# The gate of the second channel group moved into its state-space loop, two token blocks at a time

## The chip, the cores and the metric

The kernel runs on one core of a Trainium2 chip. It is one program for the core's engines: TensorE (PE, matrix products; PEld is its weight loads), VectorE (DVE), ScalarE (ACT), GpSimd (POOL), and SyncE (SP), which here only issues DMA transfers. The metric is the device time of one execution in microseconds (us); a time given for a kernel is the median of its runs.

## The reference, cut to what matters

The reference is one decoder layer over 1024 tokens of width 1024, in float32: two token mixers side by side, an output projection, a layer norm, a feed-forward part. One input projection feeds both mixers. The change is in the first mixer, a chunked state-space scan with a gate:

```
proj = x @ w_in
z, xbc, dt_raw, q, k, v, qi, ki, wi = jnp.split(proj, offsets, axis=-1)
xbc = jax.nn.silu(_causal_dwconv(xbc, ssd_conv_w, ssd_conv_b))
...
y = _ssd_scan(xs, dt, a, bm, cm)              # 8 chunks of 128 tokens, 2 groups of 8 heads
y = y + d_skip[:, None] * xs
gy = y.reshape(bsz, seqlen, SSD_INNER) * jax.nn.silu(z)
gy = gy.reshape(bsz, seqlen, SSD_GROUPS, SSD_INNER // SSD_GROUPS)
gy = gy * lax.rsqrt(jnp.mean(jnp.square(gy), axis=-1, keepdims=True) + RMS_EPS)
y_ssd = gy.reshape(bsz, seqlen, SSD_INNER) * ssd_norm_g
...
y_att = _dsa_attention(q, k, v, qi, ki, wi)   # each query attends to its 256 best keys
return jnp.concatenate([y_ssd, y_att], axis=-1) @ w_out
```

The gate is the product with silu(z) and the norm behind it. It is taken token by token, so the gate of a token block needs only the scan's result of that block; the norm needs a mean over the 512 channels of one group, for one token.

## The kernel before

A matrix product in float32 is done as three products of rounded halves (`three`, L156 to L159): an operand is split into a high part (`w_hi`) and a low part (`w_lo`). For weights of the input projection a DMA brings `w_raw`, and GpSimd computes `w_hi` (L127) and `w_lo` (L130). Results go through DRAM from stage to stage: `z_dr` holds z, `y_dr` the gated scan, `q_dr`, `k_dr`, `v_dr` the attention's operands.

The stretch that matters is the last stage of the input projection, from about 480 to 640 us. Three streams of work run in it, woven in turn, one step of each per round by `par`. The first is the plan `STAGES[4]`: the last two z tiles, the v tile (per 128-token block a `tps` product, which ScalarE brings out as `tout`), then q tiles 5, 6 and 7 in halves of 512 tokens (`proj`, brought out by ScalarE as `qkout`; tiles 6 and 7 are woven together). The second, `k_load`, starts 11 rounds late and loads the keys (`kraw`), which ScalarE and VectorE split into `kh` and `kl`. The third is the scan of the second channel group, `ssd_gen(1)`, with priority over the rest, and behind it the gate, `gate_gen(1)`.

The scan has 8 chunks of 128 tokens, here called c0 to c7, of two steps each. The first step loads a row of sums (`acsb`, a DMA); ScalarE makes the decay matrix `lmat` of it (8 relu and one exp, L523 and L525), VectorE masks it (L530), and GpSimd makes `xdt`, `xdd` and `skip`. The second does three products on TensorE (`yoff` L542, `stps` L548, `yps` L558), carries the state on (L551, L552), and VectorE writes the chunk's y (L560).

The gate goes over the 8 token blocks, b0 to b7: a DMA loads `zs` (L569), ScalarE takes silu (L570), VectorE multiplies (L572), ScalarE squares and sums (`sq`, L574). It yields after every second block. Then come the square root (L578), the reciprocal, the scaling of all 8 blocks (L582), and four steps that transpose (`yT`, L588) and store y. After the stage, the first part of the output projection starts (`ops`), with weights split by ScalarE (L129).

The order in which TensorE, VectorE, ScalarE and GpSimd take their instructions is set by a scheduler, from dependences and priorities. SP is left in the order of the program: a transfer that waits there holds every transfer behind it. Buffers come from pools with a fixed count: `xdt`, `xdd`, `skip`, `off`, `state`, `zs` and `sq` share five buffers ("s2", by `mid`), `w_raw`, `kraw`, `qraw`, `vraw` and `y_raw` share three ("wr"), and the projection products share two PSUM banks ("ip"). A transfer into a buffer waits until the last user of that buffer is through. ScalarE holds the table of one function set at a time; where exp, silu and square root follow each other, the program has an `ACT_TABLE_LOAD` between them.

Of the kernel before, what the change touches and what calls it, by code (L numbers as in the profile page):

```python
# [32 lines left out]
SSD_PRIO = 100  # L33
KDEL = 11
# [10 lines left out]
WAS = 1  # L45
TPT = ('tp', 'tp', 'ip')
QP = 2
CHAINS = (((7, "act"), (6, "dve")), ((5, "act"), (2, "act"), (4, "dve"), (3, "dve")))


# [7 lines left out]
def hybrid_layer(ctx, tc, x, w_in, ssd_conv_w, ssd_conv_b, dt_bias, a_log, d_skip, ssd_norm_g,  # L58
# [444 lines left out]
    def hv(t):  # L503
        return t.rearrange("p (h n) -> p h n", h=8)

    def ssd_gen(g, tag):
        dt, acs, eacs, cd, dd = decays
        bt, ct = bc[8 + g], bc[10 + g]
        state = None
        for c in range(NB):  # L510
            cs = slice(c * P, (c + 1) * P)
            if c % 4 == 0:
                ps = bank("btp", "tp")
                for j in range(4):
                    nc.tensor.transpose(ps[:, j * P:(j + 1) * P], bt[:, (c + j) * P:(c + j + 1) * P], ident)
                btok = mid("btok", shape=(P, 4, P))
                nc.scalar.activation(btok, ps.rearrange("p (j n) -> p j n", j=4), AF.Copy)
            ab = big("acsb", tag=tag, shape=(P, 8, P))
            nc.sync.dma_start(ab, bass.AP(tensor=a_dr.tensor, offset=a_dr.offset + (c * 16 + g * 8) * P,
                                          ap=[[0, P], [P, 8], [1, P]]))  # L520
            lm = big("lmat", tag=tag, shape=(P, 8, P))
            for h in range(8):
                nc.scalar.activation(lm[:, h, :], ab[:, h, :], AF.Relu, bias=acs[:, c, g * 8 + h:g * 8 + h + 1],  # L523
                                     scale=-1.0)
            nc.scalar.activation(lm, lm, AF.Exp, scale=-1.0)  # L525
            ps = bank("cbps", "tp")
            nc.tensor.matmul(ps[:, :P], bt[:, cs], ct[:, cs], start=True, stop=True)
            cb = small("cbm", (P, P))
            nc.vector.tensor_tensor(cb, ps[:, :P], tri, op=OP.mult)
            nc.vector.tensor_tensor(lm, lm, cb[:, None, :].to_broadcast([P, 8, P]), op=OP.mult)  # L530
            xc = xs[g][c // 2][:, c % 2, :]
            xd = [mid("xdt"), mid("xdd") if c < NB - 1 else None]
            nc.gpsimd.tensor_tensor(hv(xd[0]), hv(xc), heads(dt, g, c), op=OP.mult)
            if c < NB - 1:
                nc.gpsimd.tensor_tensor(hv(xd[1]), hv(xc), heads(dd, g, c), op=OP.mult)
            skip = mid("skip")
            nc.gpsimd.tensor_tensor(hv(skip), hv(xc), dsk[:, g * 8:g * 8 + 8][:, :, None].to_broadcast([P, 8, 64]),
                                    op=OP.mult)
            yield
            if c:  # L540
                po = bank("yoff", "lg")
                nc.tensor.matmul(po, ct[:, cs], state, start=True, stop=True)  # L542
                off = mid("off")
                nc.vector.tensor_tensor(hv(off), hv(po), heads(eacs, g, c), op=OP.mult)
                nc.gpsimd.tensor_tensor(skip, skip, off, op=OP.add)
            if c < NB - 1:
                pst = bank("stps", "lg")
                nc.tensor.matmul(pst, btok[:, c % 4, :], xd[1], start=True, stop=True)  # L548
                new = mid("state")
                if c:  # L550
                    nc.gpsimd.tensor_tensor(hv(new), hv(state), heads(cd, g, c), op=OP.mult)  # L551
                    nc.vector.tensor_tensor(new, new, pst, op=OP.add)  # L552
                else:
                    nc.vector.tensor_copy(new, pst)
                state = new
            py = bank("yps", "lg")
            for h in range(8):
                nc.tensor.matmul(py[:, h * 64:h * 64 + 64], lm[:, h, :], xd[0][:, h * 64:h * 64 + 64],  # L558
                                 start=True, stop=True)
            nc.vector.tensor_tensor(xc, py, skip, op=OP.add)  # L560
            yield


    def gate_gen(g):
        ssq = small("ssq", (P, NB))
        for b in range(NB):
            bs = slice(b * P, (b + 1) * P)
            zs = mid("zs")
            nc.sync.dma_start(zs, z_dr[bs, g * 512:g * 512 + 512])  # L569
            nc.scalar.activation(zs, zs, AF.Silu)  # L570
            y = xs[g][b // 2][:, b % 2, :]
            (nc.vector if g else nc.gpsimd).tensor_tensor(y, y, zs, op=OP.mult)  # L572
            sq = mid("sq")
            nc.scalar.activation(sq, y, AF.Square, accum_out=ssq[:, b:b + 1])  # L574
            if b % 2:
                yield
        rst = small("rst", (P, NB))
        nc.scalar.activation(rst, ssq, AF.Sqrt, bias=eps_t, scale=1.0 / 512)  # L578
        nc.vector.reciprocal(rst, rst)
        for b in range(NB):  # L580
            y = xs[g][b // 2][:, b % 2, :]
            nc.vector.tensor_scalar(y, y, rst[:, b:b + 1], None, op0=OP.mult)  # L582
        for j in range(4):
            for half in range(2):
                ps = bank("yT", "tp")
                for b in range(4):
                    bb = half * 4 + b
                    nc.tensor.transpose(ps[:, b * P:(b + 1) * P], xs[g][bb // 2][:, bb % 2, j * P:(j + 1) * P], ident)  # L588
                o = mid("qkout", tag="ev")
                nc.scalar.activation(o, ps, AF.Copy, scale=cw[:, 60 + g * 4 + j:61 + g * 4 + j])  # L590
                nc.scalar.dma_start(y_dr[(g * 4 + j) * P:(g * 4 + j + 1) * P, half * 512:half * 512 + 512], o)
            yield
# [39 lines left out]
    def k_load():  # L632
        for g in range(4):
            kr = big("kraw", tag="wr")
            for s in range(2):
                nc.sync.dma_start(kr[s * 64:s * 64 + 64], k_dr[g * 64:(g + 1) * 64, :])
            kh, kl = big("kh", F32R, tag="wo"), big("kl", F32R, tag="wo")
            nc.scalar.activation(kh, kr, AF.Copy, scale=-ATT_SCALE)
            nc.vector.scalar_tensor_tensor(kl, kr, -ATT_SCALE, f(kh), op0=OP.mult, op1=OP.subtract)
            kk_.append((kh, kl))  # L640
            yield
# [147 lines left out]
    def chain(*gens):  # L789
        for g in gens:  # L790
            yield from g

    decays = decay_gen()
    def plan_gen(plan):
        for kind, i in plan:
            if kind == "c":
                yield from conv_tile(i)
            elif kind == "q" and QP and i >= 8 - QP:
                if i == 7:
                    ws = [next_w(1 if j < QP - 1 else 0) for j in range(QP)]  # L800
                    for half in range(2):
                        for j, w in enumerate(ws):
                            yield from qk_tile(q_dr, 8 - QP + j, (half,), w)
            elif kind == "q":
                yield from qk_tile(q_dr, i)
            elif kind == "k":
                yield from qk_tile(k_dr, i)
            elif kind == "v":
                yield from tok_proj_gen(V0, AF.Copy, v_dr, 0)
            else:  # L810
                yield from tok_proj_gen(Z0 + i * 256, AF.Copy, z_dr, i * 256)

    def par(*gens):
        live = list(gens)
        while live:
            for g, n in list(live):
                try:
                    for _ in range(n):
                        yield next(g)
                except StopIteration:  # L820
                    live.remove((g, n))

    def idle(n):
        for _ in range(n):
            yield

    def prio(gen, off):
        while True:
            with tc.high_priority(off):
                try:  # L830
                    next(gen)
                except StopIteration:
                    return
            yield

    main = chain(plan_gen(STAGES[1]), par((plan_gen(STAGES[2]), 1), (prio(ssd_gen(0, "pp"), SSD_PRIO), 1)),
                 par((plan_gen(STAGES[3]), 1), (gate_gen(0), 1)),
                 par((plan_gen(STAGES[4]), 1), (chain(idle(KDEL), k_load()), 1), (chain(prio(ssd_gen(1, "pp"), SSD_PRIO), prio(gate_gen(1), SSD_PRIO)), 1)))
    weave((prio(score_gen(), 0), 1), (plan_gen(STAGES[0]), 1))
    weave((prio(topk_gen(), 0), TK), (main, MN))  # L840

# [290 lines left out]
```

## Time and profile before

| | |
|---|---|
| median of 3 runs (lowest, highest) | 1746.84 us (1745.46, 1746.99) |
| profiled execution: its time, its span | 1747.83 us, 1745.8 us |
| mean granted TensorE clock | 0.968 of full speed |
| PE, PEld busy | 1624.8 us (93%), 1346.9 us (77%) |
| DVE, ACT, POOL busy | 1192.9 us (68%), 889.3 us (51%), 801.3 us (46%) |
| chain that ended last, by engine | PE 50%, DVE 8%, issue, ACT and DMA 2% each |

The span runs from the first to the last instruction; the execution's time has 2.0 us around it. TensorE is busy for nearly the whole span, so the time is its work, its waits, and what the clock granted to it takes.

### The profile page before, as it was taken

The page shows a single profiled execution, that of the slowest core. Times are in us where ns is not written, and L with a number is a line of the kernel's source. Part 1 is how long each engine was busy: PE and PEld are TensorE (multiplying, and loading weights), DVE is VectorE, ACT ScalarE, POOL GpSimd, SP SyncE. Part 2 cuts the span into 40 slices and gives each one's busy share as a digit, 9 for nine tenths or more (in the row PEclk, how much of TensorE's full clock was granted, in tenths as well). Part 3 has the DMA queues.
Part 4 walks back from the last instruction along what each step waited for, and adds up shares of the span by engine and source line. Part 5 has one row for each costly group of instructions (what it writes and reads, how often), then busy time and mean ns, then how long its engine had stood idle before and what let it go on. Part 6 is the DMA issues. An engine that isn't in the chain of part 4 may idle for free.

```text
span 1745.8 us, 22765 instructions
## 1 busy us (share of the span) xinstructions
PE 1624.8 (93%) x7976; PEld 1346.9 (77%) x7976; DVE 1192.9 (68%) x2089; ACT 889.3 (51%) x1625; POOL 801.3 (46%) x560
## 2 busy tenths in 40 slices
PE   7899998998998699999999977999999999899997
PEld 5688887776897568777787755888888888688886
DVE  3533779999368477787777478887887786515516
ACT  3333597687632476666666344544444443333231
POOL 2222234634265254545454348755555552445351
PEclk9999999999999889999999987999999999899999
DMA  5122022131333464454553551222222223446443
GB/s 168 38 79 67 27 92 88 43 115 52 125 103 91 151 202 127 127 167 118 162 147 124 171 169 60 85 94 76 77 84 93 85 73 115 139 145 229 157 153 125
DMA packets 180938, 198.22 MB, mean 114 GB/s; under 512 B 12003, under 2 KB 136279, under 8 KB 180823
## 3 DMA queue, kind: packets, MB, share of 16 engines
q1 hardware_dynamic: 147351, 145.37, 28.1%
q10 hardware_dynamic: 33472, 51.39, 8.1%
q8 instruction: 63, 1.03, 0.3%
q14 instruction: 52, 0.43, 0.1%
HBM read 145.28 MB, written 51.45 MB: 113 GB/s over the span
## 4 chain that ended last, share of the span: by engine, by line
PE 50%; DVE 8%; issue 2%; ACT 2%; DMA 2%; POOL 0%; ACTq 0%; DVEq 0%; POOLq 0%; SPq 0%
PE acc L157 5%; PE acc L159 5%; PE acc L158 5%; PE ops L157 3%; PE ops L158 3%; PE ops L159 3%; PE ptp L689 3%; PE pc L157 2%; PE pc L158 2%; PE pc L159 2%; PE pa L157 2%; PE pd L158 2%; PE pd L157 2%; PE pd L159 2%; PE pa L158 2%
## 5 line engine op out<-in xcount | busy, mean ns | idle before, releaser
L130 POOL TENSOR_TENSOR w_lo<-w_raw,w_hi 128x1024 fp32r<-128x1024 f32 (+1 forms) x89 | 222.0, 2500 | 162.5 <-ACT w_hi L129 160.3
L157 PE MATMUL proj<-xTh,w_hi 128*128 128x512 f32 (+1 forms) x432 | 174.1, 403 | 18.3 <-POOL w_hi L127 6.6
L159 PE MATMUL proj<-xTh,w_lo 128*128 128x512 f32 (+1 forms) x432 | 173.1, 402 | 2.8 <-POOL w_lo L130 2.8
L158 PE MATMUL proj<-xTl,w_hi 128*128 128x512 f32 (+1 forms) x432 | 174.6, 404 | 0.0
L997 POOL TENSOR_TENSOR w_hl<-s,w_hl 128x512 fp32r<-128x512 f32 x88 | 129.1, 1472 | 83.8 <-ACT w_hl L996 83.5
L683 POOL TENSOR_SCALAR prob<-prob,sm 128x512 f32<-128x512 f32 (+7 forms) x128 | 96.3, 763 | 139.7 <-DVE sm L682 109.9
L1075 DVE TENSOR_TENSOR g_hl<-g_raw,g_hl 128x512 fp32r<-128x512 f32 x44 | 62.0, 1422 | 131.4 <-ACT g_hl L1074 131.4
L997 POOL TENSOR_TENSOR w_hl<-w_raw,w_hl 128x512 fp32r<-128x512 f32 x66 | 105.4, 1599 | 88.3 <-ACT w_hl L996 57.9
L157 PE MATMUL acc<-w_hi,g_hl 128*128 128x512 f32 x352 | 136.3, 395 | 7.8 <-ACT g_hl L1074 7.8
L158 PE MATMUL acc<-w_lo,g_hl 128*128 128x512 f32 x352 | 137.7, 391 | 0.0
L159 PE MATMUL acc<-w_hi,g_hl 128*128 128x512 f32 x352 | 137.6, 391 | 0.0
L127 POOL TENSOR_SCALAR w_hi<-w_raw 128x1024 fp32r<-128x1024 f32 x35 | 40.0, 1143 | 172.1 <-PE proj L158 135.6
L680 ACT ACTIVATE prob<-prob,mx 128x512 f32<-128x512 f32 (+7 forms) x128 | 98.4, 771 | 35.9 <-DVE mx L677 35.7
L691 ACT ACTIVATE pt<-ptp 128x512 fp32r<-128x512 f32 x144 | 81.1, 594 | 64.3 <-PE ptp L689 43.7
L157 PEld LDWEIGHTS proj<-xTh,w_hi 128*128 128x128 f32 (+1 forms) x432 | 83.1, 192 | 37.9 <-issue 7.1
L157 PE MATMUL ops<-w_hi,y_hi 128*128 128x512 f32 x256 | 103.7, 405 | 3.1 <-ACT y_hi L129 3.1
L692 DVE TENSOR_TENSOR pt<-ptp,pt 128x512 fp32r<-128x512 f32 x144 | 95.5, 684 | 15.6 <-ACT pt L691 15.2
L158 PE MATMUL ops<-w_lo,y_hi 128*128 128x512 f32 x256 | 102.6, 401 | 0.4 <-DVE w_lo L130 0.4
L353 ACT ACTIVATE junk<-score,cand 128x1024 bf16<-128x1024 f32 (+2 forms) x96 | 85.9, 895 | 32.4 <-DVE cand L367 30.6
L129 ACT ACTIVATE w_hi<-w_raw 128x1024 fp32r<-128x1024 f32 (+1 forms) x62 | 65.1, 1052 | 72.8 <-PE acc L159 48.1
L159 PE MATMUL ops<-w_hi,y_lo 128*128 128x512 f32 x256 | 101.2, 398 | 0.0
L157 PE MATMUL tps<-w_hi,xTh 128*128 128x256 f32 x320 | 95.1, 298 | 3.6 <-ACT tout L611 2.1
(314 smaller groups left out, 4788.9 us busy)
## 6 DMA issues: line engine op xcount, KB each, us to landing
w_raw<-in_ffn_w_up_dram SPq DMA_DIRECT2D x44, 512.0 KB, 3.9
w_raw<-in_ffn_w_down_dram SPq DMA_DIRECT2D x44, 512.0 KB, 3.7
w_raw<-in_w_in_dram SPq DMA_DIRECT2D x36, 512.0 KB, 4.8
r_dr<-rout ACTq DMA_DIRECT2D x48, 256.0 KB, 2.1
g_dr<-vg ACTq DMA_DIRECT2D x22, 512.0 KB, 2.6
g_raw<-g_dr SPq DMA_DIRECT2D x44, 256.0 KB, 4.0
acsb<-a_dr SPq DMA_DIRECT2D x16, 512.0 KB, 4.0
w_raw<-in_w_out_dram SPq DMA_DIRECT2D x16, 512.0 KB, 4.6
```

The source lines that it names most:

```text
L129: nc.scalar.activation(hi, raw, AF.Copy)
L130: (nc.vector if lo_on_dve else nc.gpsimd).tensor_tensor(lo, raw, f(hi), op=OP.subtract)
L157: nc.tensor.matmul(ps, ah, bh, start=start, stop=False, skip_group_check=onto)
L158: nc.tensor.matmul(ps, ah, bl, start=False, stop=False, skip_group_check=onto)
L159: nc.tensor.matmul(ps, al, bh, start=False, stop=stop, skip_group_check=onto)
L353: nc.scalar.activation(junk[1][:, :n], score_ap[b], AF.Sign, bias=c, scale=-1.0, accum_out=val[e][:, i:i + 1])
L680: nc.scalar.activation(t[:, :w], t[:, :w], AF.Exp, bias=mx[:, h:h + 1], scale=-1.0, accum_out=sm[:, h:h + 1])
L683: nc.gpsimd.tensor_scalar(t[:, :w], t[:, :w], sm[:, 4 + h:5 + h], 1.0, op0=OP.mult, op1=OP.mult)
L691: nc.scalar.activation(pt[:, 0], ps, AF.Copy)
L692: nc.vector.tensor_tensor(pt[:, 1], ps, f(pt[:, 0]), op=OP.subtract)
L997: nc.gpsimd.tensor_tensor(t[:, 1], src, f(t[:, 0]), op=OP.subtract)
L1075: nc.vector.tensor_tensor(t[:, 1], raw, f(t[:, 0]), op=OP.subtract)
```

## The change

`ssd_gate` takes the place of the chain of scan and gate in the last stage. It counts the scan's 16 steps from 0 (chunk c is steps 2c and 2c+1) and puts a gate step of two blocks behind steps 9, 10, 12 and 15: blocks b0, b1 behind the second step of c4, b2, b3 behind the first step of c5, b4, b5 behind the first step of c6, and b6, b7 at the end. What is left of the gate follows as before. Each gate step put in takes a round, so the steps of c5, c6 and c7 come one, two and three rounds later beside the plan.

```diff
+GATE_AT = (9, 10, 12, 15)
...
+    def ssd_gate(g):
+
+        gates = prio(gate_gen(g), SSD_PRIO)
+        for n, _ in enumerate(prio(ssd_gen(g, "pp"), SSD_PRIO)):
+            yield
+            if n in GATE_AT:
+                next(gates)
+                yield
+        yield from gates
+
...
-                 par((plan_gen(STAGES[4]), 1), (chain(idle(KDEL), k_load()), 1), (chain(prio(ssd_gen(1, "pp"), SSD_PRIO), prio(gate_gen(1), SSD_PRIO)), 1)))
+                 par((plan_gen(STAGES[4]), 1), (chain(idle(KDEL), k_load()), 1), (ssd_gate(1), 1)))
```

The work is the same, but for table loads: the before has one load for silu and one for the square root in this gate; the change has four for silu, three more for the exps of c5 to c7 between them, and the one for the square root, six more in all. Lines of the changed kernel are one higher than before, and buffer numbers differ.

Queue SP before, from the load of c5's `acsb` to the weights of q tile 7 (`acsb_4769`, `_4957`, `_5142` are c5, c6, c7; `w_raw_4980`, `_5163`, `_5253` the weights of q5, q6, q7; `zs_5241`, `_5247` are b0, b1):

```order
L519 DMA acsb_4769<-a_dr_103 128x1024
L636 DMA kraw_4848<-k_dr_97 64x1024 x2
L636 DMA kraw_4950<-k_dr_97 64x1024 x2
L519 DMA acsb_4957<-a_dr_103 128x1024
L138 DMA w_raw_4980<-in_w_in_dram 128x8x128
L636 DMA kraw_5042<-k_dr_97 64x1024 x2
L636 DMA kraw_5135<-k_dr_97 64x1024 x2
L519 DMA acsb_5142<-a_dr_103 128x1024
L138 DMA w_raw_5163<-in_w_in_dram 128x8x128
L569 DMA zs_5241<-z_dr_102 128x512
L569 DMA zs_5247<-z_dr_102 128x512
L138 DMA w_raw_5253<-in_w_in_dram 128x8x128
```

Queue SP with the change, from the same place to the weights of q6 (`zs_4770`, `_4776` are b0, b1, `zs_4950`, `_4956` b2, b3; `acsb_4845`, `_5124` c5, c6; `w_raw_4962`, `_5147` q5, q6):

```order
L570 DMA zs_4770<-z_dr_102 128x512
L570 DMA zs_4776<-z_dr_102 128x512
L637 DMA kraw_4838<-k_dr_97 64x1024 x2
L520 DMA acsb_4845<-a_dr_103 128x1024
L637 DMA kraw_4943<-k_dr_97 64x1024 x2
L570 DMA zs_4950<-z_dr_102 128x512
L570 DMA zs_4956<-z_dr_102 128x512
L139 DMA w_raw_4962<-in_w_in_dram 128x8x128
L637 DMA kraw_5024<-k_dr_97 64x1024 x2
L637 DMA kraw_5117<-k_dr_97 64x1024 x2
L520 DMA acsb_5124<-a_dr_103 128x1024
L139 DMA w_raw_5147<-in_w_in_dram 128x8x128
```

The loads of b0 and b1 now stand ahead of c5's `acsb`, and those of b2 and b3 ahead of the weights of q5. By the buffers that the pool gives out, b0's load waits for the y of c4 (the last reader of a `skip`), b1's for the square of b0, b2's for the `yps` products of c5 (the last readers of an `xdt`), and b3's for the product of b2. On TensorE the `yps` of c5 are the last instructions ahead of q5's first product.

ScalarE before, around the v tile's blocks 2 to 5 (`tout_4900` to `tout_5039`), where c7's `lmat` is made; those of c5 and c6 stand further ahead:

```order
L638 ACTIVATE kh_4851<-kraw_4848 128x1024
L611 ACTIVATE tout_4900<-tps_4875 128x256
L612 DMA v_dr_101<-tout_4900 128x256
L611 ACTIVATE tout_4928<-tps_4903 128x256
L612 DMA v_dr_101<-tout_4928 128x256
L611 ACTIVATE tout_5011<-tps_4986 128x256
L612 DMA v_dr_101<-tout_5011 128x256
L523 ACTIVATE lmat_5144<-acsb_5142,dtset_655 128x128 x8
L611 ACTIVATE tout_5039<-tps_5014 128x256
L525 ACTIVATE lmat_5144<-lmat_5144 128x1024
```

ScalarE with the change at the v tile's blocks 4 to 6 (`tout_4993` to `tout_5086`), where c5's `lmat` is made:

```order
L575 ACTIVATE sq_4774,ssq_4769<-xs_3530 128x512
L612 ACTIVATE tout_4993<-tps_4968 128x256
L571 ACTIVATE zs_4776<-zs_4776 128x512
L613 DMA v_dr_101<-tout_4993 128x256
L575 ACTIVATE sq_4780,ssq_4769<-xs_3530 128x512
L639 ACTIVATE kh_4841<-kraw_4838 128x1024
L612 ACTIVATE tout_5021<-tps_4996 128x256
L524 ACTIVATE lmat_4847<-acsb_4845,dtset_655 128x128 x8
L613 DMA v_dr_101<-tout_5021 128x256
L612 ACTIVATE tout_5086<-tps_5061 128x256
L526 ACT_TABLE_LOAD
L526 ACTIVATE lmat_4847<-lmat_4847 128x1024
```

The gate of b0 and b1 and the split of the first keys now stand ahead of two `tout` and of c5's `lmat`, and a table load ahead of its exp.

TensorE with the change at the end of q tile 7 (`proj_5379` is its last half; `yT_5418` the first transposes of the gated y; in the kernel before all of these transposes stand behind the last `proj`):

```order
L158 MATMUL proj_5379<-xTh_112,w_hi_5243 128x512
L589 MATMUL yT_5418<-ident_80,xs_3530 128x128
L159 MATMUL proj_5379<-xTl_120,w_hi_5243 128x512
L589 MATMUL yT_5418<-ident_80,xs_3530 128x128
L160 MATMUL proj_5379<-xTh_112,w_lo_5244 128x512
L589 MATMUL yT_5418<-ident_80,xs_3531 128x128
L158 MATMUL proj_5379<-xTh_112,w_hi_5243 128x512
```

ScalarE ahead of the `qkout` that frees the bank for that last half (`zs_5367`, `_5373` are b6, b7; the change):

```order
L571 ACTIVATE zs_5367<-zs_5367 128x512
L575 ACTIVATE sq_5371,ssq_4769<-xs_3533 128x512
L571 ACTIVATE zs_5373<-zs_5373 128x512
L130 ACTIVATE w_hi_5484<-w_raw_5482 128x1024
L130 ACTIVATE w_hi_5490<-w_raw_5488 128x1024
L130 ACTIVATE y_hi_5497<-y_raw_5494 128x1024
L575 ACTIVATE sq_5377,ssq_4769<-xs_3533 128x512
L579 ACT_TABLE_LOAD
L579 ACTIVATE rst_5407<-ssq_4769,eps_94 128x8
L462 ACTIVATE qkout_5321<-proj_5296 128x512
```

The gate's end has moved up among the last products of q7, and that `qkout` now stands behind it; in the kernel before it stands ahead of b5's silu.

## Rows read from the trace of the kernel before

**Rows 1.** Two stretches: busy PE, PEld, DVE, ACT, POOL; clock; DMA.

```profile
520.00:553.00 33.00, 28.46 (x216) 26.78 (x215) 30.98 (x58) 8.48 (x19) 18.07 (x11) 0.95 0.35 96
...
608.00:617.00 9.00, 8.50 (x23) 5.85 (x24) 7.17 (x10) 3.94 (x5) 2.37 (x2) 0.53 0.74 191
```

**Rows 2.** TensorE's waits, 540 to 640 us: releaser, total, times, longest.

```profile
PE yT L588 <- DVE xs L582: 7.0, 2, 6.6
...
PE yoff L542 <- DVE state L552: 4.5, 1, 4.5
...
PE lgps L674 <- DVE mx L677: 1.8, 1, 1.8
```

**Rows 3.** Timeline of queue SP: start, length of the row, transfer, count.

```profile
487.34 0.32 SPq L519 DMA_DIRECT2D acsb<-a_dr  x1
...
522.48 0.39 SPq L138 DMA_DIRECT2D w_raw<-in_w_in_dram  x1
```

**Rows 4.** DMA issues, 480 to 640 us: count, size, median us to landing.

```profile
acsb<-a_dr SPq DMA_DIRECT2D x4, 512.0 KB, 4.0
w_raw<-in_w_in_dram SPq DMA_DIRECT2D x4, 512.0 KB, 4.2
...
zs<-z_dr SPq DMA_DIRECT2D x8, 256.0 KB, 2.9
...
y_raw<-y_dr SPq DMA_DIRECT2D x4, 256.0 KB, 5.7
```

**Rows 5.** Timeline of ScalarE: start, length, instruction, idle before it.

```profile
545.28 2.45 ACT L523 ACTIVATE lmat<-acsb,dtset 128x128 f32<-128x128 f32 x8 [10.20 <-DMA acsb<-a_dr]
...
547.90 1.04 ACT L525 ACTIVATE lmat<-lmat 128x1024 f32<-128x1024 f32 x1
...
550.19 0.39 ACT L611 ACTIVATE tout<-tps 128x256 f32<-128x256 f32 x1 [1.25 <-PE tps L159]
...
551.04 1.06 ACT L638 ACTIVATE kh<-kraw 128x1024 fp32r<-128x1024 f32 x1 [0.46 <-ACT tout L611]
...
576.58 1.28 ACT L570 ACT_TABLE_LOAD   x1 [4.56 <-DMA zs<-z_dr]
577.88 0.63 ACT L570 ACTIVATE zs<-zs 128x512 f32<-128x512 f32 x1
579.33 0.63 ACT L574 ACTIVATE sq<-xs 128x512 f32<-128x512 f32 x1 [0.82 <-DVE xs L572]
```

**Rows 6.** Timeline of VectorE: the y of c4, the mask of c7.

```profile
532.37 0.68 DVE L560 TENSOR_TENSOR xs<-yps,skip 128x512 f32<-128x512 f32 x1
...
548.97 1.23 DVE L530 TENSOR_TENSOR lmat<-lmat,cbm 128x1024 f32<-128x1024 f32 x1 [0.44 <-ACT lmat L525]
```

**Rows 7.** Groups of VectorE, 520 to 622 us: the gate's products.

```profile
L572 DVE TENSOR_TENSOR xs<-xs,zs 128x512 f32<-128x512 f32 x8 | 6.2, 772 | 22.9 <-ACT zs L570 22.9
```

**Rows 8.** Groups of GpSimd, 520 to 600 us: weights' halves, state.

```profile
L130 POOL TENSOR_TENSOR w_lo<-w_raw,w_hi 128x1024 fp32r<-128x1024 f32 x4 | 10.1, 2528 | 0.2
...
L551 POOL TENSOR_TENSOR state<-state,dtset 128x512 f32<-128x512 f32 x3 | 4.6, 1529 | 0.0
L127 POOL TENSOR_SCALAR w_hi<-w_raw 128x1024 fp32r<-128x1024 f32 x3 | 4.4, 1480 | 9.7 <-DMA w_raw<-in_w_in_dram 9.2 <-PE proj L159 0.6
```

**Rows 9.** Timeline of TensorE at the start of q5.

```profile
552.87 0.40 PE L157 MATMUL proj<-xTh,w_hi 128*128 128x512 f32 x1
553.11 0.40 PE L158 MATMUL proj<-xTl,w_hi 128*128 128x512 f32 x1
```

**Rows 10.** Timeline of TensorE at its wait for q7's weights.

```profile
582.25 0.80 PE L157 MATMUL proj<-xTh,w_hi 128*128 128x512 f32 x1 [6.56 <-POOL w_hi L127]
...
585.40 0.54 PE L159 MATMUL proj<-xTh,w_lo 128*128 128x512 f32 x1
```

**Rows 11.** Timeline of TensorE: the gate's end, the first attention product.

```profile
608.06 0.48 PE L588 MATMUL yT<-ident,xs 128*128 128x128 f32 x1 [6.60 <-DVE xs L582]
...
620.44 0.36 PE L674 MATMUL lgps<-kh,qst 128*128 128x256 f32 x1
```

## The prediction

> **What bounds the kernel now.** TensorE sets the time, so I read first what it waits for in the stage that the change touches, then who is late behind each wait. The table of TensorE's waits [rows 2] gives 7.0 us for the scaling at the gate's end (6.6 in one piece), 4.5 for the scan's state, 1.8 for a maximum of the attention. The timeline has one more of that size: q7's first product starts at 582.25 after 6.56 us for its `w_hi` [rows 10]. The first one ends at 608.06 with the first `yT` [rows 11], and the first attention product follows at 620.44. Each of these two waits also costs clock. From 582.25 to 585.40 eight products of one size start, seven intervals in 3.15 us [rows 10], 0.45 each where q5's first two, at full speed, are 0.24 apart [rows 9]; that is 1.5 us lost. From 608 to 617 TensorE was granted 0.53, half speed, while it was busy for 8.5 us [rows 1], so about 4.0 of them would not have been needed at full clock.
>
> The gate's end is late because its first `zs` only comes at 576: ScalarE idles 4.56 us for it, then loads the silu table [rows 5]. That is what an earlier gate can win. What it can lose stands in queue SP. Today the load of c5's `acsb` goes out at 487.34 and q5's weights at 522.48 [rows 3], while q5's first product starts at 552.87 without a wait [rows 9]. Thirty microseconds of lead hide the weights' way completely.
>
> **What is taken away.** The gate's tail: 7.0 of waiting and 4.0 of clock, 11.0. The wait for q7's weights: they now stand in the queue behind b0's and b1's loads, which wait for buffers; in the change those are long gone, so 6.6 and 1.5 of clock, 8.1. Together 19.1 us. I take both as gone, which the order supports: the `yT` products are now woven into the last `proj`.
>
> **What is put in ahead of q5.** The new order of SP chains q5's weights to c5's `yps`, by way of b2's load (which takes a buffer that those products read) and b3's (which waits for the product of b2). I follow it from c4's y, which VectorE ends at 533.05 [rows 6]. One mask of `lmat`, 1.23 [rows 6], leaves the stretch ahead of it, so 531.8. b0's load lands 2.9 later [rows 4]; table 1.28, silu 0.63 [rows 5]: 536.6. The product takes 0.77 [rows 7], but VectorE is busy 30.98 of 33 us here with the masks of the top-k [rows 1], and today's trace shows no gate product in that crowd. Its wait there lies between nothing and 5 us (about four of the instructions that the order puts ahead of it, each like the 1.23 of rows 6); I take 3. Then the square, 0.63 [rows 5]: 541.0, and only then b1's load goes out. Two key loads and c5's `acsb` follow, each near the 0.32 to 0.39 of an issue [rows 3]: `acsb` leaves at 542.3, 55 us later than today, and lands 4.0 later [rows 4] at 546.3. ScalarE does not reach it yet: b1 lands at 544.1, silu 0.63, the product 3.8 with its wait, the square 0.63, `kh` 1.06, a `tout` 0.39 [rows 5], which gives 550.6. Eight relu 2.45, another `tout` 0.39, table 1.28, exp 1.04 [rows 5] and the mask 1.23 [rows 6] end at 557.0. Behind that come c5's `yps`, which are short and left out.
>
> From there one chain, with no other work of TensorE ahead of q5: b2's load 2.9 [rows 4], table 1.28 and silu 0.63 [rows 5], product 0.77 [rows 7], b3's issue 0.32 [rows 3], the weights' landing 4.2 [rows 4], `w_hi` 1.48 [rows 8]. That is 11.6, so q5 starts at 568.6 and not at 552.87: **15.7 us later**. With the two product waits at nothing it is 9.7, at 5 each 19.7. The 4.5 us wait for the state [rows 2] lies ahead of this and is inside 15.7: a chain, not TensorE, sets the start, so whether it shrinks does not matter.
>
> A wait as long as the one at 582.25 costs clock behind it as there, 1.5 [rows 10]. And q5's `w_lo` now stands on GpSimd behind the state's pass, 1.53, and one like it (`skip`), itself 2.53 [rows 8]: 5.6 us behind `w_hi`. TensorE has five products to do until it needs it (four of q5 and the `yoff` of c6), 2.3 at 0.45; 3.3 is left. Nothing of the kind is seen today; the bounds are nothing and 5.6.
>
> **The price of the tables.** Six more loads are 7.7 us of ScalarE at 1.28 [rows 5], of which the two ahead of c5's exp and b2's silu are on the path and already in the sum. Silu follows its load at 577.88, right where 576.58 and 1.28 end [rows 5]: nothing is lost behind it. The Trainium skill ("ScalarE: Activation LUTs", section "What ACT_TABLE_LOAD costs") gives 1283 ns for the load, as measured here, and adds a drain of 1380 ns to each switch, which this trace does not show; by the next section ("Table sets: the hidden batching unit") calls should be grouped by set, which speaks against this change. With the page's drain on the two loads the sum would be 2.8 us longer; I leave it out.
>
> **What is put in at the end.** The last half of q7 needs the bank of a `qkout` which now stands on ScalarE behind b6, b7, three splits, the last square, the root's table and the root. From the issue of b7's load it is: y's landing 5.7 [rows 4], its split 1.0 (as the `kh` of equal size), square 0.63, table 1.28 [rows 5], and about 1.5 of issues and small ones, some 10 us, of which the products of q6 and q7 that are still to do cover some. Bounds are nothing and 10; TensorE has only the other three halves to hide it, so I take 6, with 2 for the clock behind it (between the 1.5 and the 4.0 above). One more us for q7's own weights, whose loads now stand closer to their use: 9.0.
>
> Further on, the 1.8 us wait for the attention's maximum [rows 2] may shrink, since VectorE has had the time to finish what is ahead of it: −1.
>
> **The sum.** 15.7 + 1.5 + 3.3 − 19.1 + 9.0 − 1.0 = +9.4. On the profiled execution (span 1745.8, time 1747.83) it gives 1757.2. That execution is 1.0 above the median of the runs, so for a median I say **1756**.
>
> **The rivals.**
> - *Bigger loss.* VectorE makes both products wait 5 (+4.0), and the end costs its full 10 (+4): +17, or about 1764. For it: VectorE's crowd and three streams that now end on one engine, ScalarE. Against it: the masks thin out by 550. Chance 0.13.
> - *Even.* VectorE takes the products at once, q5 is 9.7 late, the rest as above: +3.4, about 1750. It needs a gate product to slip into a stretch where VectorE is 94% busy; the gate's priority speaks for it. Between this and the forecast lies everything from +3 to +9. Chance that it ends within 0.2% (3.5 us, about what a measurement of this kernel can tell from no change): 0.15.
> - *Faster.* The end costs nothing, because a q5 that is 10 to 16 us late gives ScalarE and VectorE the time to do the keys, the masks and the gate's first six blocks beside TensorE's idle time. Place: the `qkout` ahead of q7's last half. Price: 9.0 less. With q5 at 9.7 the total is 9.7 + 1.5 + 3.3 − 19.1 − 1.0 = −5.6, about 1741; with q5 at 15.7 it is +0.4. It decides only where q5's delay stays under 11.8 us (a total of −3.5) with an end that is free. For it: the whole gain of 19.1 is real in today's trace. Against it: the order puts the root's table and three waits for DMA ahead of that `qkout`. Chance of faster by over 0.2%: 0.14.
> - That the change does nothing is no case: the order of SP, ScalarE and TensorE shows it done.
>
> **The numbers.** Slower by over 0.2% has 0.71, of which the forecast's own range, 1751 to 1761, is most. The range from 1744 to 1763 leaves about one in ten on each side: below, the faster rival at its best; above, the bigger loss.
>
> **What would show it.** Right: in the new trace queue SP issues q5's weights after 555, right behind b3's load; TensorE has one wait of 9 to 13 us for `w_hi` ahead of q5, and q5 starts between 563 and 573; half clock follows it; the wait of 6.6 for the scaling is gone, as is that for q7's weights; a wait for `qkout` of some us stands ahead of q7's last half. Wrong: q5's weights issued before 545, or a first attention product that starts before 620.44 [rows 11]; in the first case the buffer waits resolved earlier than followed here, in the second the end cost nothing.

## The result and the profile after

The change is slower: 1756.97 us (median of 4 runs, 1754.93 to 1760.53) against 1746.26 us before, a ratio of 1.0063, 95% interval 1.0049 to 1.0077. That is 10.7 us more. The profiled execution took 1756.44 us with a span of 1754.5, 8.7 more than the span before, at the same mean clock (0.967 against 0.968). The prediction was 1756, from +9.4 on the profiled execution.

Queue SP of the change in order of time (start, length, transfer, count), which answers to [rows 3]:

```profile
531.35 6.52 SPq L570 DMA_DIRECT2D zs<-z_dr  x2
...
539.22 0.53 SPq L520 DMA_DIRECT2D acsb<-a_dr  x1
...
557.39 5.82 SPq L570 DMA_DIRECT2D zs<-z_dr  x2
563.26 0.43 SPq L139 DMA_DIRECT2D w_raw<-in_w_in_dram  x1
```

c5's `acsb` goes out at 539.22, not at 487.34, and q5's weights at 563.26, not at 522.48. The first stands two key loads behind a pair of `zs`, the second right behind one, and each pair takes about 6 us in the queue: the second load goes out only when the first block is through.

TensorE's waits in the change, 540 to 640 us (total, times, longest), to be read against [rows 2]:

```profile
PE proj L158 <- POOL w_hi L128: 12.2, 2, 11.9
PE proj L158 <- ACT qkout L462: 7.4, 2, 7.1
PE yps L559 <- DVE lmat L531: 4.8, 1, 4.8
...
PE proj L160 <- POOL w_lo L131: 0.7, 1, 0.7
```

The wait for the scaling at the gate's end (7.0) and that for q7's weights (6.56) are gone. In their place stand 11.9 us for q5's `w_hi` and 7.1 for a `qkout`. The timeline of TensorE gives the first its place:

```profile
553.65 3.67 PE L559 MATMUL yps<-xdt,lmat 128*128 128x64 f32 x16 [4.85 <-DVE lmat L531]
569.18 0.79 PE L158 MATMUL proj<-xTh,w_hi 128*128 128x512 f32 x1 [11.86 <-POOL w_hi L128]
...
571.05 2.00 PE L543 MATMUL yoff<-state,conv 128*128 128x512 f32 x2
573.74 0.50 PE L160 MATMUL proj<-xTh,w_lo 128*128 128x512 f32 x1 [0.69 <-POOL w_lo L131]
574.07 0.39 PE L158 MATMUL proj<-xTh,w_hi 128*128 128x512 f32 x1
```

The `yps` products of c5 end at 557.3. b2's load goes out at 557.39, and q5 starts at 569.18 [rows 9: 552.87], at about half clock until 574 (0.43 from product to product; granted clock 0.53 from 569 to 574, 1.00 from 574 to 580).

### The profile page after: what moved, and what is told of

It is laid out like the page before. It is cut to its first block, busy times and chain, and to the rows that moved or that the text cites. A ratio compares the mean times of both kernels' runs of the same rounds, so it can differ in the third digit from the quotient of the medians.

```text
span 1754.5 us, 22769 instructions
## 1 busy us (share of the span) xinstructions
PE 1624.2 (93%) x7976; PEld 1345.8 (77%) x7976; DVE 1190.4 (68%) x2089; ACT 897.6 (51%) x1631; POOL 801.2 (46%) x560
## 4 chain that ended last, share of the span: by engine, by line
PE 65%; DVE 19%; issue 5%; ACT 5%; DMA 4%; POOL 1%; SPq 1%; ACTq 0%; DVEq 0%; POOLq 0%
PE acc L158 5%; PE acc L160 5%; PE acc L159 5%; DVE junk L351 4%; PE proj L158 3%; PE proj L159 3%; PE proj L160 3%; PE ops L158 3%; PE ops L159 3%; PE ops L160 3%; PE ptp L690 3%; PE pc L158 2%; PE pd L158 2%; PE pd L159 2%; PE pc L159 2%
## 5 line engine op out<-in xcount | busy, mean ns | idle before, releaser
L158 PEld LDWEIGHTS proj<-xTh,w_hi 128*128 128x128 f32 (+1 forms) x432 | 83.3, 193 | 51.0 <-POOL w_hi L128 12.8
```

Of the source, the lines that this page charges most:

```text
L158: nc.tensor.matmul(ps, ah, bh, start=start, stop=False, skip_group_check=onto)
```

## The experiments

Each kernel was timed beside the kernel before; the ratio is to the runs of that kernel on the same chip. Line numbers are those of the change where nothing else is said.

**Undo one place in the queue.** q5's weights are loaded two blocks earlier in the v tile, which puts them ahead of b2 and b3:

```diff
-            if b == 4:
+            if b == (2 if c0 == V0 else 4):
                 load_ahead(1)
```

> The change with one thing undone: q5's weights are loaded two token blocks earlier in the v tile, so that in the queue SP they stand ahead of the loads of b2 and b3. Theory Q (the queue: q5's weights are held behind loads that wait for c5's yps): the wait of 11.9 us ahead of q5 is gone, q5 starts right behind c5's yps at about 557, with full clock; some of it comes back as a wait for q6's weights (still behind kraw and b3, out at about 575, wanted about 10 us earlier than now), so 5 to 11 us less than the change: 1746 to 1752 us, ratio to before 1.000 to 1.003. Theory A (ScalarE is overloaded by table loads and by gate rows ahead of evictions): nothing on ScalarE has changed, so the time stays within 3 us of the change, 1754 to 1760, and the 11.9 us come back as waits for ScalarE.

1756.57 us, ratio 1.0058 (1.0036 to 1.0079): no measurable part came back. The weights were on time (538.32 in the rows of SP) and q5 started at 550.25. But then the next thing in line waited. SP and TensorE of this kernel, start, length, and the idle time before:

```profile
538.32 0.42 SPq L139 DMA_DIRECT2D w_raw<-in_w_in_dram  x1
...
559.59 5.76 SPq L570 DMA_DIRECT2D zs<-z_dr  x2
```

```profile
550.25 0.40 PE L158 MATMUL proj<-xTh,w_hi 128*128 128x512 f32 x1
...
574.71 1.22 PE L543 MATMUL yoff<-state,conv 128*128 128x512 f32 x1 [9.71 <-DVE state L553]
```

VectorE of the same kernel, and below it GpSimd:

```profile
564.30 0.69 DVE L573 TENSOR_TENSOR xs<-xs,zs 128x512 f32<-128x512 f32 x1 [4.78 <-ACT zs L571]
568.42 0.69 DVE L573 TENSOR_TENSOR xs<-xs,zs 128x512 f32<-128x512 f32 x1 [3.42 <-ACT zs L571]
569.21 0.69 DVE L545 TENSOR_TENSOR off<-yoff,dtset 128x512 f32<-128x512 f32 x1
...
573.98 0.68 DVE L553 TENSOR_TENSOR state<-state,stps 128x512 f32<-128x512 f32 x1
```

```profile
570.05 1.26 POOL L546 TENSOR_TENSOR skip<-skip,off 128x512 f32<-128x512 f32 x1 [15.69 <-DVE off L545]
571.27 1.04 POOL L552 TENSOR_TENSOR state<-state,dtset 128x512 f32<-128x512 f32 x1
```

c6's `yoff` waits 9.71 us for the state of c5. VectorE has that state's row (573.98) behind the products of b2 and b3 (564.30 and 568.42), and GpSimd's pass over the state (571.27) stands behind a `skip`, for which GpSimd sat idle for 15.69 us until VectorE had made `off`, behind those products. b2's load is still held until c5's `yps` are through. So the queue theory was right about the place of the wait and wrong about its cause: work that waits for the pair of loads stands in VectorE's order too, and through it in GpSimd's, and whoever is next in line pays for it. Theory A did forecast the time (within 3 us of the change), but its waits for ScalarE did not come: the wait is for VectorE. A small gain was there for a while: the attention's last product starts at 983.35, 2.8 us earlier than in the change, and that is lost again at the start of the feed-forward part (more on this stretch below, under the sum).

**Table loads alone.** relu in place of silu in this gate; the output leaves out silu, and the order on the engines stays the same but for the table loads:

```diff
-            nc.scalar.activation(zs, zs, AF.Silu)
+            nc.scalar.activation(zs, zs, AF.Silu if g == 0 else AF.Relu)
```

> The change, with relu in place of silu in the gate of the second channel group (this leaves silu out, so the output is not the reference's): all orders of instructions stay the same, seven table loads of 1.28 us are gone from ScalarE. Theory A: most of their 9.0 us comes back, 1748 to 1750. Theory Q: only those that lie on the chain count, ahead of c5's exp and b2's silu, and at the end the one ahead of b6's silu, 2.6 to 3.9 us: 1753 to 1754.5; the wait ahead of q5 shrinks from 11.9 to 10.6.

1754.19 us, ratio 1.0046 (1.0029 to 1.0063), 2.8 less than the change: as theory Q said, and not the 7 to 9 of theory A, whose 1748 to 1750 lie below the interval. The 2.8 by themselves are not clear of noise (the change has 1.0049 to 1.0077). TensorE's two long waits shrank by 1.6 and 1.4 us, about one table load each:

```profile
PE proj L158 <- POOL w_hi L128: 10.3, 1, 10.3
PE proj L158 <- ACT qkout L462: 6.0, 2, 5.7
```

**Later places.**

```diff
-GATE_AT = (9, 10, 12, 15)
+GATE_AT = (9, 12, 14, 15)
```

> The change with other places for the gate's steps: 9, 12, 14, 15 in place of 9, 10, 12, 15, so b2 and b3 come a chunk later, behind q5's weights in the queue but ahead of q6's. Theory Q: q5 starts without the long wait, and a wait of some us appears ahead of q6 instead, since its weights now stand behind b2 and b3, which wait for buffers: 3 to 9 us less than the change, 1748 to 1754. Theory A: nearly as many table loads and the same gate rows: within 3 us of the change, 1754 to 1760.

1754.22 us, ratio 1.0045 (1.0032 to 1.0059). The time lies at the edge of what each theory gave; the waits say more. q5 started at 552 after a 2.0 us wait, q6's weights did not cause a long one, and this stood in its place:

```profile
PE yoff L543 <- DVE state L553: 12.3, 2, 10.1
PE yps L559 <- DVE lmat L531: 5.4, 2, 5.1
```

10.1 us in one piece for a state, 5.1 for a mask: the round trips of b2 and b3 as in the first experiment, one chunk later.

**One gate step only.**

```diff
-GATE_AT = (9, 10, 12, 15)
+GATE_AT = (9,)
```

> The change with only the first gate step (b0, b1, behind c4) inside the loop, the other six blocks behind it as before. Theory Q: the 11.9 us ahead of q5 are gone, as b2 and b3 no longer stand ahead of its weights; b0 and b1 still stand ahead of c5's acsb, so the 4.8 us wait for c5's mask stays; the gate's tail comes back in part (6 blocks instead of 8, so some 2 to 4 us less of the 6.6 before): 1745 to 1751. Theory A: two extra table loads instead of six: a third of the 10.7 us loss, 1749 to 1751 too; apart from Q it keeps a wait for ScalarE rather than none at q5.

1750.74 us, ratio 1.0027 (1.0014 to 1.0039). Inside the range of both. q5 waits 2.7 us for `w_hi`. The tail did not come back shorter than the 6.6 of before, as theory Q had it, but longer, as a wait for `y_hi`, which ScalarE makes behind the last six blocks (the profiled execution took 1754.29, 3.6 above the median):

```profile
PE ops L158 <- ACT y_hi L130: 9.7, 1, 9.7
```

**Loads ahead, in buffers of their own.** After the first four runs the theory was widened to the round trips themselves. Two buffers ("gz") for the `zs` of this gate, for which one of two `cbm` buffers goes, and each pair loaded one step ahead:

```diff
+        def z_load(b):
+            zq.append(mid("zs", tag="gz" if g else "s2"))
+            nc.sync.dma_start(zq[-1], z_dr[b * P:(b + 1) * P, g * 512:g * 512 + 512])
...
             if b % 2:
+                if g and b < NB - 1:
+                    z_load(b + 1)
+                    z_load(b + 2)
                 yield
...
-GATE_AT = (9, 10, 12, 15)
+GATE_AT = (8, 9, 10, 12, 15)
```

> After e1 the theory is wider, theory L (latency): a gate step in the loop is a chain of two loads, one after the other, each a round trip from DMA over ScalarE and VectorE, and whichever engine's queue it stands in pays for it, q5's weights in the change, c5's state in e1. Here the gate steps stay where the change has them, but each load goes out one gate step ahead into two buffers of its own (for which one buffer of cbm goes). Theory L: the round trips are gone from all queues, no wait over 4 us is left between 530 and 605, and the gain at the gate's end stays: 5 to 11 us less than before, 1735 to 1741. Theory P (the place itself: gate rows and table loads between the scan's rows delay c5 to c7, loads or not): the waits ahead of q5 or of the state stay over half, 1750 to 1757.

1744.72 us, ratio 0.999 (0.9978 to 1.0001): some 12 us less than the change, but not faster than before by any measurable amount. No wait over 4 us is left between 530 and 605, as theory L said, but its time was missed by some 4 us. In its queue the loads of a pair ahead wait for their buffers and hold q7's weights behind them:

```profile
549.95 15.49 SPq L571 DMA_DIRECT2D zs<-z_dr  x2
565.53 0.39 SPq L139 DMA_DIRECT2D w_raw<-in_w_in_dram  x1
```

But TensorE has no wait for a `w_hi` in this trace, so this is not what it lost. The last `proj` product starts at 604.28, 1.8 us earlier than in the kernel with spread places below (606.09), the last row of `yT` at 631.97, 7.0 later than there (624.94): the loss lies at the gate's end, with waits for the scaling (5.0 in two) and, at 621.16, for a `qkout`. Why they are longer here was not tested.

```profile
PE yT L602 <- ACT qkout L604: 4.1, 1, 4.1
```

**Six shared buffers.**

```diff
-    S2, EV = 5, 2
+    S2, EV = 6, 2
```

> The change with six s2 buffers for five and nothing else: b1's load then waits for the product of b0 and no longer for its square, b3's for a mask and for xdd and no longer for b2's product; b2's still waits for c5's yps. Theory L: b3's load goes out with b2's, so one of the two round trips behind c5's yps falls away, 4 to 5 us less ahead of q5: 1750 to 1754. Theory P: within 3 us of the change.

1750.89 us, ratio 1.0026 (1.0015 to 1.0037), some 6 us less than the change, as theory L said, but not quite by its mechanism: in its timeline of SP b2 and b3 still take 5.2 us (from 546.86, where the change has 557.39), and the whole chain is 10 us earlier, since the first pair got out at 520.62 and not at 531.35.

**Preloads at the old place, and at other places.** The kernel with preloads, once with the gate behind the scan (first pair loaded behind step 13) and once with a step behind the second half of each chunk:

```diff
-GATE_AT = (8, 9, 10, 12, 15)
+GATE_AT = (13,)
```

> The gate back behind the scan as before, but with loads one step ahead into buffers of their own (the first pair behind step 13). It tells what the place gives beside what the loads give. Theory L: ScalarE's 4.56 us for the first zs and the queue's wait go, the gate's end comes up to 5 us earlier, and q7's weights are no longer held: 4 to 9 us less than before, 1737 to 1742. Theory P (the place is what matters, loads are cheap): same as before within 3 us.

1736.98 us, ratio 0.9955 (0.9939 to 0.997).

```diff
-GATE_AT = (8, 9, 10, 12, 15)
+GATE_AT = (8, 9, 11, 13, 15)
```

> As the one with preloads, but with the gate's steps at 9, 11, 13 and 15, each behind the second step of a chunk. Theory L: as there, 1735 to 1741, since no queue waits for a load in either. Theory P: better than there by over 3 us, as fewer gate rows stand ahead of c5's and c6's second steps.

1736.02 us, ratio 0.9948 (0.9931 to 0.9965). Both beat the kernel before. Theory P is right on one point: the same preloads at 9, 11, 13 are 8.7 us faster than at 9, 10, 12. Its reason, fewer gate rows ahead of c5 and c6, is not shown by this.

**Buffers without preloads.** To part the two edits: buffers of their own, loads where the change has them.

```diff
-            zs = mid("zs")
+            zs = mid("zs", tag="gz" if g else "s2")
```

> The change with two zs buffers of its own for this gate (one cbm buffer goes for them) and the loads where the change has them, none ahead. It parts the two things that the preloads changed together. Theory B (the wait for a buffer of the shared five is what makes the round trips long and late): b0 to b3 load early, no wait for w_hi ahead of q5, most of the loss is gone: 1740 to 1748. Theory O (the order, a load standing behind the step before it, is what costs; buffers alone do little): 1749 to 1755.

1736.29 us, ratio 0.9938 (0.9921 to 0.9955), faster than theory B had it, and with no load ahead. Queue SP of this kernel:

```profile
487.64 7.72 SPq L570 DMA_DIRECT2D zs<-z_dr  x2
...
501.61 7.13 SPq L570 DMA_DIRECT2D zs<-z_dr  x2
522.42 0.38 SPq L139 DMA_DIRECT2D w_raw<-in_w_in_dram  x1
```

The loads of b0 to b3 go out between 487 and 509, and q5's weights at 522.42, where they were before the change (522.48). No wait for `w_hi` is left, and the longest waits are these:

```profile
PE yoff L543 <- DVE state L553: 7.2, 2, 4.6
PE yT L589 <- ACT qkout L591: 4.4, 2, 3.5
```

**Two controls.** All kernels with buffers of their own also have one `cbm` buffer fewer, so this edit was run by itself, in the kernel before and in the change:

```diff
-            cb = small("cbm", (P, P))
+            cb = small("cbm", (P, P), bufs=1)
```

> The kernel before with one buffer of cbm for two, which all kernels with buffers of their own have. Theories B and O both expect no difference to before beyond 3 us, 1743 to 1749; if it is faster by more, the preloads' gains are owed to it in part.

1740.83 us, ratio 0.9965 (0.9949 to 0.9982): 5.6 us faster than before, which neither theory expected. In its trace the two waits that the prediction wanted to win with an early gate have shrunk by themselves, from 6.6 and 7.0, and a wait of 6.3 us for a `y_hi` has come:

```profile
PE proj L157 <- POOL w_hi L127: 2.2, 1, 2.2
...
PE yT L588 <- DVE xs L582: 0.8, 1, 0.8
```

> The change with one buffer of cbm for two and nothing else: the control for the three kernels that have buffers of their own at places inside the loop, after the control at the old place gave 5.6 us by itself. Its queue still makes b1, b2 and b3 wait as in the change. Theory B (buffers of their own give the gain at these places): the wait for w_hi ahead of q5 stays over 8 us and the time within 6 us of the change, 1749 to 1757. Theory C (the gain is that of cbm): 1735 to 1742, and no long wait ahead of q5.

1752.89 us, ratio 1.0042 (1.0028 to 1.0056), as theory B said, with the long wait still there:

```profile
PE proj L158 <- POOL w_hi L128: 12.5, 2, 11.8
```

So at the change's places the buffers, and not `cbm`, take the ratio from 1.0042 to 0.9938. Against the kernel before on the same chip (1745.28 and 1746.38) that is from 7.6 us slower to 10.1 faster, 17.7 us. At the old place it is otherwise:

> The kernel before, the gate behind the scan, with two zs buffers of its own and no load ahead. Theory B: as fast as the one with preloads at the old place, 1735 to 1740, since the first loads go out as soon as the queue reaches them and q7's weights no longer wait behind them. Theory O: same as before within 3 us.

1739.56 us, ratio 0.9954 (0.9937 to 0.9972), against 0.9965 with the `cbm` edit alone. Buffers of their own give nothing that can be measured there, and the gain over before is that of `cbm`; so is nearly all of that of the preloads at the old place (0.9955). With the gate behind the scan and these buffers, the waits for q7's weights and for the scaling are gone altogether, and one for a `qkout` stands in their place:

```profile
PE proj L157 <- ACT qkout L461: 8.3, 1, 8.3
```

## Why the prediction was right, point by point

**The chain to q5: right in size, by errors that cancel.** Predicted 15.7 us later, measured 569.18 − 552.87 = 16.3. VectorE and ScalarE of the change on the way:

```profile
530.59 0.68 DVE L561 TENSOR_TENSOR xs<-yps,skip 128x512 f32<-128x512 f32 x1
...
536.06 0.69 DVE L573 TENSOR_TENSOR xs<-xs,zs 128x512 f32<-128x512 f32 x1
...
541.05 0.69 DVE L573 TENSOR_TENSOR xs<-xs,zs 128x512 f32<-128x512 f32 x1 [1.15 <-ACT zs L571]
...
552.37 1.22 DVE L531 TENSOR_TENSOR lmat<-lmat,cbm 128x1024 f32<-128x1024 f32 x1 [2.50 <-ACT lmat L526]
```

```profile
535.40 0.63 ACT L571 ACTIVATE zs<-zs 128x512 f32<-128x512 f32 x1
...
540.39 0.63 ACT L571 ACTIVATE zs<-zs 128x512 f32<-128x512 f32 x1 [2.60 <-DMA zs<-z_dr]
...
547.26 0.40 ACT L524 ACTIVATE lmat<-acsb,dtset 128x128 f32<-128x128 f32 x1 [2.49 <-DMA acsb<-a_dr]
```

c4's y ends at 531.27 (531.8 taken). The two products start at 536.06 and 541.05, each within 0.03 us of the end of its silu: the 3 us of waiting that I took for each, because VectorE was crowded, did not exist, 6.0 us less. But c5's `acsb` went out at 539.22 and ScalarE could start on it only at 547.26, 8.0 later and not 4.0 as in [rows 4]; ScalarE was idle for the last 2.49 of them, so 2.5 us more. With the mask done at 553.59, 3.4 earlier than followed, c5's `yps` then took 3.7 us at a granted clock of 0.50, which I had left out as short (16 of them took 1.89 us in the kernel before, at 547.02). Together that is −6.0 + 2.5 + 3.7 = +0.2: that the start of q5 came out within 0.6 us is luck. From b2's load to q5 it is 11.8 us, 11.6 predicted, and this part of the chain was right.

**Behind q5.** Wait for `w_lo` and half clock were taken as 3.3 + 1.5. From 569.18 to 574.07 seven products start in 4.9 us, which at 0.23 would take 1.6: 3.3 lost in all, of which 0.69 is `w_lo`. So `w_lo` was mis-sized: it was ready 4.6 us behind q5's start and not 5.6, and the work ahead of it took 3.9 us and not 2.3, since the `yoff` is two products and took 2.00 at half clock.

**The end.** Predicted 6 of waiting, 2 of clock, 1 for q7's weights. ScalarE ahead of the `qkout`:

```profile
605.90 0.63 ACT L571 ACTIVATE zs<-zs 128x512 f32<-128x512 f32 x1 [1.94 <-DMA zs<-z_dr]
608.34 1.06 ACT L130 ACTIVATE w_hi<-w_raw 128x1024 fp32r<-128x1024 f32 x1 [1.81 <-DMA w_raw<-in_w_out_dram]
609.91 1.06 ACT L130 ACTIVATE w_hi<-w_raw 128x1024 fp32r<-128x1024 f32 x1 [0.52 <-DMA w_raw<-in_w_out_dram]
611.46 1.06 ACT L130 ACTIVATE y_hi<-y_raw 128x1024 fp32r<-128x1024 f32 x1 [0.49 <-DMA y_raw<-y_dr]
612.42 0.61 ACT L575 ACTIVATE sq<-xs 128x512 f32<-128x512 f32 x1
...
613.15 1.28 ACT L579 ACT_TABLE_LOAD   x1
614.44 0.30 ACT L579 ACTIVATE rst<-ssq,eps 128x8 f32<-128x8 f32 x1
614.65 1.06 ACT L462 ACTIVATE qkout<-proj 128x512 f32<-128x512 f32 x2
```

and TensorE behind it:

```profile
615.28 0.80 PE L158 MATMUL proj<-xTh,w_hi 128*128 128x512 f32 x1 [7.07 <-ACT qkout L462]
...
621.42 0.42 PE L160 MATMUL proj<-xTh,w_lo 128*128 128x512 f32 x1
...
630.37 0.36 PE L675 MATMUL lgps<-kh,qst 128*128 128x256 f32 x1
```

Silu of b7, three splits (each behind its DMA), square, table, root, `qkout`: it ran as the order had it, and TensorE waited 7.07. Then 14 products at 0.43 instead of 0.23 (granted clock 0.50 from 615 to 621.4), 2.8 lost. q7's weights, a `yoff` and another `qkout` cost 0.36, 1.00 and 0.28.

**The sum at the first attention product.** 630.37 against 620.44 [rows 11], 9.9 us. The terms as measured (16.3 + 3.3 − 19.1 + 9.9 + 1.6) give 12.0; the other 2.1 were not broken down. But it is not the same point of the work in both: 21 of the gate's 32 transposes had run by then before, and 11 in the change. The attention's last product (`pv`) is a better one (the kernel before, then the change):

```profile
973.42 0.39 PE L695 MATMUL pv<-pt,v 128*128 128x512 f32 x1
986.19 0.39 PE L696 MATMUL pv<-pt,v 128*128 128x512 f32 x1
```

There the change is 12.8 us later. Its span is only 8.7 longer, so 4.1 came back behind the attention, 3.6 of them at the start of the feed-forward part, from 1030 to 1064 in the kernel before, where VectorE was busy for 31.18 of 34.00 us and TensorE for 17.14. TensorE is likely not what sets the time there. The prediction has no such term: its 1.0 was for a wait in the attention, which shrank by 0.8 (2.2 to 1.4 between 600 and 720). That the time came out within 1 us of the 1756 is in part luck.

**The rivals.** "Even" needed products that VectorE takes at once, and that did happen, but it needed the loads and the `yps` at their usual length too. "Faster" needed an end that costs nothing; it cost 9.9. The signs named for being right all came: q5's weights out after 555 (563.26), one wait of 9 to 13 us for `w_hi` (11.86), half clock behind it, the two old waits gone, and one for a `qkout` ahead of q7's last half (7.07).

**What was wrong in the reasoning.** The prediction followed the loads through their buffers, but charged them to one place, q5's weights behind them in queue SP. The first experiment took that place away and the time did not move. What costs is the pair of loads that share five buffers with the scan, and so can start only when c5's products are through, one after the other: 17.7 us, from the change with the `cbm` edit to the same with two buffers of their own (the orders that the scheduler makes differ between these two, and were not held fixed). And the 19.1 us taken away were put down to the early gate, but the two waits in them go without it too: they shrink with one `cbm` buffer fewer, and are gone with two buffers for `zs` at the old place. Whether an early gate is worth anything once it does not wait is not settled: 0.9938 and 0.9948 inside the loop against 0.9954 and 0.9955 behind the scan, some 3 us apart at most, with intervals that overlap. Nor is it known why the preloads at 9, 10, 12 are slower than at 9, 11, 13, or than the same buffers without preloads.

The table load cost what its row says: the root starts at 614.44, 0.01 us behind the end of the load at 613.15. The Trainium skill ("ScalarE: Activation LUTs", section "What ACT_TABLE_LOAD costs") adds a drain of about 1380 ns to each switch; the rows here do not show it. The time without seven loads, 2.8 us less, fits two on the path at 1.28, but its interval is too wide to rule the drain out by itself.

## What to carry to other kernels

When a step is moved earlier, follow the buffers that it takes, not only its data: a load that shares a pool with the stage it is moved into can start no earlier than that stage lets go, and it stands then at the head of an in-order queue. Undoing one place where it hurt only moved the wait to the next in line here; taking the cause away (4 KB of buffers per partition) left no wait over 5 us in this stretch. Compare at the end of a stretch as well as at the end of the kernel: a later stage can hide part of a loss. And control each edit that comes along with an experiment: here a buffer taken away elsewhere was worth 5.6 us by itself.

## What was not expected

One `cbm` buffer fewer makes the kernel before 5.6 us faster (0.9965, interval 0.9949 to 0.9982). The order that the scheduler makes is another one in many places, and q7's weights go out at 570.56 and not at 576.15; why the one edit leads to that is open. And a load's landing is no constant: `acsb` of the same 512 KB took 3.8 to 8.0 us from issue to landing over the changed kernel, the longest being the one on the path.
